# A feed-forward layer in two phases, its inner operands kept in DRAM between, both products by seven block products

## The chip, the cores and the metric

The kernel runs on one core of a Trainium2 chip. The metric is the device time of one launch in microseconds (us), median of the runs. Engines: TensorE (PE, with its weight load PEld), VectorE (DVE), ScalarE (ACT), GpSimd (POOL) and SyncE (SP), which issues all transfers here.

## The reference

One step of a streaming encoder layer on 1024 prompt rows and 64 sample rows (T = 1088 columns), width D = 1024, inner width 4096:

```
z  = x @ w_in
merged = sigmoid(g_A) * y_A + sigmoid(g_B) * y_B     # conv branch, mLSTM branch
x1 = LN(ALPHA * x + merged @ w_out)
ff = square(relu(x1 @ w_ff1)) @ w_ff2                # w_ff1 1024x4096, w_ff2 4096x1024
x2 = LN(ALPHA * x1 + ff)
```

Everything is fp32. Only the feed-forward (the line of `ff`) is changed.

## The kernel before

A product in fp32 is made of three matmuls on operands split into a high and a low part (`mm3`, lines 342, 345, 346: high·high, high·low, low·high). `split` (L350, L353; with a scale L355, L356) makes the parts: ScalarE copies the high part, VectorE takes the difference as the low part. Activations lie with features on the partitions and the 1088 columns in three chunks of 384, 384 and 320. `x1` is held split (X1H, X1L), the kept sum for the second norm is `Y2`, one tile a chunk.

A *unit* is 128 inner features: `unit` makes for each chunk 8 products (24 matmuls) and passes the result to a function `post`. A list of jobs (`J` with a weight piece, `N` without) is worked off in order; `wload` issues a weight piece two jobs ahead, `wsplit` splits it one job ahead. A scheduler then places the instructions on each engine in an order of its own; each engine, and SyncE with its transfers, runs strictly in that order and waits where an operand is not there.

The feed-forward goes over 8 blocks of four units. In blocks 0 to 6, four units of x1 @ w_ff1 (`post_r`: relu, square, and the seven sums that the second product needs, split, kept in SBUF) are followed by the second product for these 512 inner features by seven block products in place of eight (`wino_pair`): operands are cut into halves, sums of halves of weights (`wino_weights`) and of activations are multiplied, and VectorE adds the results into `Y2`. Four passes `jp` over the output features give 4 × 7 × 2 × 2 × 3 = 336 matmuls of 272 columns a block. Both products of a block so alternate with the next block's. Block 7 is classical: `post_h` keeps its four units in SBUF, `y2_turn` transposes `Y2` (L1084, 72 transposes), and `last_ff2` makes the products of 512 columns with the rows as partitions, with the second norm (`ln2_back`) and the stores. The first norm `ln1` runs chunk by chunk beside the first units (`ln_feature`, L744, L745, L748); `first_units` works chunk-wise so that the units can begin before the norm's last chunk is there.

## Time and profile before

| | |
|---|---|
| Time, median of 3 runs | 1944.36 us (1944.29 to 1945.13) |
| The profiled execution | 1945.67 us, span 1943.9 us, TensorE clock 0.998 |
| TensorE busy | 1922.5 us (99%), 12396 matmuls |
| VectorE / ScalarE / GpSimd busy | 1390.9 / 638.1 / 124.0 us |
| Moved by DMA | 131.06 MB, mean 67 GB/s |
| First unit of the feed-forward | from 1191.56 us |
| First block of the second product | 1240.63 to 1286.44 us |

A row of the groups is: line, engine, operation, output<-inputs, shapes, count | busy us, mean ns of one | idle time of the engine just before them, and the releaser that ended most of it. A row of the timeline begins with its start and its duration in us; the bracket at its end is the idle time before it and what ended it. A row of the windows is a stretch, its length, and for PE, PEld, DVE, ACT and POOL the busy time and the count of instructions, then the granted TensorE clock, the DMA share and GB/s. The rows of GB/s and of PEclk cut their stretch into 40 equal slices.

### The profile page before, as it was taken

How to read it: one execution, taken by the hardware profiler on the slowest of the kernel's cores; microseconds unless marked ns; L12 is line 12 of the kernel's file. 1: busy time of each engine (PE TensorE's matmuls, PEld its weight loads, DVE VectorE, ACT ScalarE, POOL GpSimd, SP SyncE). 2: the span in 40 equal slices, each digit the busy share in tenths (PEclk: the TensorE clock that was granted, in tenths of full speed). 3: DMA queues.
4: the chain of work that ended last, by engine and by line, in shares of the span. 5: the costliest groups of instructions: out<-in, count | busy, mean ns of one | idle time of the engine just before them, and what ended most of it. 6: DMA issues, size and time to landing. Idle time of an engine off the chain costs nothing.

```text
span 1943.9 us, 30514 instructions
## 1 busy us (share of the span) xinstructions
PE 1922.5 (99%) x12396; PEld 1902.4 (98%) x12396; DVE 1390.9 (72%) x2735; ACT 638.1 (33%) x1204; POOL 124.0 (6%) x229
## 2 busy tenths in 40 slices
PE   8999999999999999999999999999999999999998
PEld 8999999999999999999999999999999999999996
DVE  4957876787678867877775557868685858677647
ACT  4323322332233223323452214523233232414242
POOL 1112210001000100000000000000000000000005
PEclk9999999999999999999999999999999999999999
DMA  4121311122112211226335211011111111111212
GB/s 144 53 80 52 124 53 53 51 72 57 56 33 68 73 56 44 61 88 198 104 111 155 77 39 39 23 55 45 55 42 46 55 44 47 41 55 44 73 37 92
DMA packets 171744, 131.06 MB, mean 67 GB/s; under 512 B 8271, under 2 KB 166463, under 8 KB 171603
## 3 DMA queue, kind: packets, MB, share of 16 engines
q1 hardware_dynamic: 171603, 129.11, 21.9%
q8 instruction: 97, 1.59, 0.3%
q14 instruction: 44, 0.36, 0.1%
HBM read 104.39 MB, written 24.63 MB: 66 GB/s over the span
## 4 chain that ended last, share of the span: by engine, by line
PE 94%; DVE 4%; DMA 1%; ACT 0%; issue 0%; POOL 0%; DVEq 0%; SPq 0%; POOLq 0%; ACTq 0%
PE g L342 29%; PE g L345 29%; PE g L346 29%; PE m L342 1%; PE m L346 1%; PE m L345 1%; DVE acc L586 1%; PE m L480 0%; PE m L1084 0%; PE m L427 0%; DVE wl L353 0%; PE m L486 0%; PE m L464 0%; DMA x<-in_x_prompt_dram 0%; PE m L169 0%
## 5 line engine op out<-in xcount | busy, mean ns | idle before, releaser
L342 PE MATMUL g<-xh,wh 128*128 128x384 f32 (+1 forms) x1920 | 634.9, 331 | 0.0
L345 PE MATMUL g<-xl,wh 128*128 128x384 f32 (+1 forms) x1920 | 628.9, 328 | 0.9 <-DVE xl L174 0.9
L346 PE MATMUL g<-xh,wl 128*128 128x384 f32 (+1 forms) x1920 | 628.6, 327 | 0.0
L345 PEld LDWEIGHTS g<-xl,wh 128*128 128x128 f32 x1920 | 361.4, 188 | 1.3 <-DVE xl L174 1.2
L342 PEld LDWEIGHTS g<-xh,wh 128*128 128x128 f32 x1920 | 361.3, 188 | 0.7 <-ACT xh L173 0.3
L346 PEld LDWEIGHTS g<-xh,wl 128*128 128x128 f32 x1920 | 361.0, 188 | 0.1
L586 DVE SCALAR_TENSOR_TENSOR acc<-glu,vecs,acc 128x1118 f32<-128x1118 f32 x240 | 332.4, 1385 | 3.6
L350 ACT ACTIVATE wh<-wr 128x1024 fp32r<-128x1024 f32 (+1 forms) x168 | 165.9, 988 | 440.4 <-PE g L345 358.5
L353 DVE TENSOR_TENSOR wl<-wr,wh 128x1024 fp32r<-128x1024 f32 (+1 forms) x168 | 192.7, 1147 | 97.4 <-ACT wh L350 94.5
L342 PE MATMUL g<-x1h,wh 128*128 128x384 f32 (+1 forms) x768 | 252.8, 330 | 0.0
L345 PE MATMUL g<-x1l,wh 128*128 128x384 f32 (+1 forms) x768 | 252.2, 328 | 0.0
L346 PE MATMUL g<-x1h,wl 128*128 128x384 f32 (+1 forms) x768 | 252.1, 328 | 0.0
L345 PE MATMUL g<-hvl,wh 128*128 128x272 f32 x784 | 224.3, 289 | 0.0
L342 PE MATMUL g<-hvh,wh 128*128 128x272 f32 x784 | 221.8, 291 | 1.5 <-DVE y L995 1.5
L346 PE MATMUL g<-hvh,wl 128*128 128x272 f32 x784 | 222.4, 289 | 0.0
L997 DVE TENSOR_TENSOR y<-g,y 128x272 f32<-128x272 f32 (+1 forms) x540 | 156.9, 339 | 28.1 <-PE g L346 26.3
L342 PEld LDWEIGHTS g<-hvh,wh 128*128 128x128 f32 x784 | 146.5, 190 | 3.4 <-DVE y L995 1.9
L345 PEld LDWEIGHTS g<-hvl,wh 128*128 128x128 f32 x784 | 148.1, 189 | 0.0
L346 PEld LDWEIGHTS g<-hvh,wl 128*128 128x128 f32 x784 | 147.1, 189 | 0.0
L345 PEld LDWEIGHTS g<-x1l,wh 128*128 128x128 f32 x768 | 144.3, 188 | 0.1
L342 PEld LDWEIGHTS g<-x1h,wh 128*128 128x128 f32 x768 | 144.2, 188 | 0.1
L346 PEld LDWEIGHTS g<-x1h,wl 128*128 128x128 f32 x768 | 144.3, 188 | 0.0
(276 smaller groups left out, 2359.2 us busy)
## 6 DMA issues: line engine op xcount, KB each, us to landing
wr<-in_w_in_dram SPq DMA_DIRECT2D x64, 512.0 KB
wr<-in_w_ff_dram SPq DMA_DIRECT2D x64, 512.0 KB
x<-in_x_prompt_dram SPq DMA_DIRECT2D x8, 512.0 KB
dwT<-acc SPq DMA_DIRECT2D x8, 512.0 KB
wr<-in_w_b_out_dram SPq DMA_DIRECT2D x8, 512.0 KB
wr<-in_w_a_out_dram SPq DMA_DIRECT2D x8, 512.0 KB
wr<-in_w_out_dram SPq DMA_DIRECT2D x8, 512.0 KB
out_dram<-o SPq DMA_DIRECT2D x16, 256.0 KB
```

What stands on the lines that cost most here:

```text
L342: first = TE.matmul(out, lh, rh, start=start, stop=False, skip_group_check=more)
L345: TE.matmul(out, lh, rl, start=False, stop=False, skip_group_check=more)
L346: TE.matmul(out, ll, rh, start=False, stop=stop, skip_group_check=more)
L350: a = S.activation(hi, src, AF.Copy)
L353: V.tensor_tensor(lo, src, hi.bitcast(F32), ALU.subtract)
L586: V.scalar_tensor_tensor(acc, glu[:, j:j + AC], vecs[:, c, j:j + 1], acc, ALU.mult, ALU.add))
L997: V.tensor_tensor(y, ps[:, pslc], y, ALU.add)
```

## The change

The feed-forward is no longer worked off in blocks that do both products.

- The four classical units (28 to 31) come first; `post_h` writes their two parts to DRAM (`hidD`). `ln1` also writes `Y2`, X1H and X1L to DRAM (`y1D`, `x1D`).
- `x1_sums` makes the four sums of column halves and row blocks of x1 that seven products need, split: six pieces of four sums, four copies and four lows, interleaved with the last chunk's work.
- `ff_first` makes the 28 other units in 14 rounds of seven block products, each 24 matmuls of 272 columns. The three plain operands come back from `x1D`. Weights of a round are loaded raw (1 MB, one buffer), and summed and split form by form (`item`) into nine slots. `stream` sets the order: a round's last three products (P6, P7, P4) stand between the next round's first ones. `done` takes results out of PSUM, makes relu and square, and the seven operands of the second product in two parts, written to DRAM (`hvD`, 14 tiles of 128x544 a round).
- All of that memory is given back; `ff_second` then makes 28 rounds (7 blocks × 4 passes `jp`) of seven products, 84 matmuls of 272 columns each. The operands of a block are read back from `hvD` (14 loads, two blocks' worth of buffers), the kept sum stays in SBUF (`YF`, from `y1D`). `last_ff2` transposes `YF` row tile by row tile between its products, its weights and `hidD` come in during block 5.

The diff, cut to its core:

```diff
-    for blk in range(NBLK - 1):
-        for kt in range(2):
-            for kh in range(2):
-                c0 = (blk * NB + 2 * kh + kt) * P
-                if blk == 0 and kt == 0:
-                    J(wcols(w_ff1[0], c0), lambda hi, lo, kh=kh: first_units(kh, hi, lo), "f" if kh else "w")
-                else:
-                    add_unit(w_ff1[0], c0, lambda *a, kt=kt, kh=kh: post_r(kt, kh)(*a))
-        for jp in range(KT // 2):
-            wino_pair(blk, jp)
...
-    N(open_last)
-    for u in range((NBLK - 1) * NB, NBLK * NB):
-        add_unit(w_ff1[0], u * P, post_h(u))
-    N(last_ff2)
...
+    y1D = dram.tile([D, T], F32, name="y1D")
+    x1D = [dram.tile([D, T], F32, name=f"x1D{e}") for e in "hl"]
+    hidD = [dram.tile([4 * P, T], F32, name=f"hidD{e}") for e in "hl"]
+    hvD = dram.tile([14 * 7 * 2 * P, 544], F32, name="hvD")
...
         yield from ln_feature(Y2[ci], n, pools["ln1"], square, finish, ((2, 3, 2), (1, 3, 1), (1, 2, 1))[ci], YS[ci])
+        o = CHUNKS[ci][0]
+        for dst, src in ((y1D, Y2[ci]), (x1D[0], X1H[ci].bitcast(F32)), (x1D[1], X1L[ci].bitcast(F32))):
+            nc.sync.dma_start(dst[:, o:o + n].rearrange("(k p) t -> p k t", p=P), src[:, :, :n])
...
+    VN = ("b11", "b21", "b22", "t1", "t2", "t3", "t4")
+    USES = {"P1": ("a11", "b11"), "P2": ("a12", "b21"), "P3": ("s4", "b22"), "P5": ("s1", "t1"), "P6": ("s2", "t2"),
+            "P7": ("s3", "t3"), "P4": ("a22", "t4")}
+    BANK = {"P1": "a", "P6": "a", "P7": "a", "P4": "a", "P5": "b", "P3": "b", "P2": "c"}
...
+    def ztile(name):
+        zq.append(0)
+        return pools["hvs1" if len(zq) % 14 < 4 or "hvs2" not in pools else "hvs2"].tile([P, HT2], F32R, tag="z", name=name)
...
+            r, hi = ztile("r"), ztile("rh")
+            rf = r.bitcast(F32)
+            S.activation(rf[:, :n], ps[:, :n], AF.Relu)
+            V.scalar_tensor_tensor(rf[:, :n], ps[:, :n], 0.0, rf[:, :n], ALU.max, ALU.mult)
+            split(hi[:, :n], r[:, :n], rf[:, :n])
+            for e, t in enumerate((hi, r)):
+                nc.sync.dma_start(hidD[e][u * P:(u + 1) * P, o:o + n], t.bitcast(F32)[:, :n])
...
+    def x1_sums():
...
+        for a, b, ca, oa, cb, ob in ((0, 224, 0, 0, 1, 160), (224, 384, 0, 224, 2, 0), (384, 544, 1, 0, 2, 160)):
+            n = b - a
+            for i in range(2):
...
+                V.tensor_tensor(z[0], b11, b12, ALU.subtract)
+                keep("t1", z[0])
+                V.scalar_tensor_tensor(z[1], z[0], -1.0, b22, ALU.mult, ALU.subtract)
+                keep("t2", z[1])
+                V.tensor_tensor(z[0], b22, b12, ALU.subtract)
+                keep("t3", z[0])
+                V.scalar_tensor_tensor(z[1], z[1], -1.0, b21, ALU.mult, ALU.subtract)
+                keep("t4", z[1])
+                yield
...
+        if u == 1:
...
                 unit(*h, (1,))
             early[1] = product(*his[third], 1)
             drain("misc")
+            BG["misc"].append(x1_sums())
+            step("misc")
...
+    N(open_ff)
+    for u in range(4):
+        c0 = (4 * KT - 4 + u) * P
+        if u < 2:
+            J(wcols(w_ff1[0], c0), lambda hi, lo, u=u: first_units(u, hi, lo), "f" if u else "w")
+        else:
+            add_unit(w_ff1[0], c0, post_h(u))
...
+    def stream(n, weight, operand, nk, done, between=None):
...
+            for sg in range(2):
+                for k in range(nk):
+                    bh, bl = operand(q, bn, k, slice(sg * HB, (sg + 1) * HB))
+                    mm3(ps[:, sg, :HB], *weight(q, an, k), bh, bl, nm in ("P1", "P2", "P5") and k == 0, k == nk - 1, more=True)
+            done(q, nm, {k: bank.get((q, k)) for k in "abc"})
+
+        for q in range(n + 1):
+            for nm in ("P6", "P1", "P7", "P5", "P4", "P2", "P3"):
+                old = nm in ("P6", "P7", "P4")
+                if 0 <= q - old < n:
+                    run(q - old, nm)
+                    if between:
+                        between(q - old, nm)
...
+    def ff_first():
...
+        for i, (nm, kh, th) in enumerate((("b11", 0, 0), ("b22", 1, 1), ("b21", 1, 0))):
...
+                nc.sync.dma_start(t.bitcast(F32), x1D[e].rearrange("(i b p) t -> b p i t", b=2, p=P)[kh][:, :, th * HT2:(th + 1) * HT2])
...
+        ws = [fp.tile([P, 3072], F32R, tag="f", name="wv") for _ in range(3)]
+        order = ("a11", "s1", "a12", "s4", "s2", "s3", "a22")
...
+        def produce():
+            for q in range(NQ):
+                raw = pools["rawp"].tile([P, 2 * KT * P], F32R, tag="raw", name="raw").bitcast(F32)
+                nc.sync.dma_start(raw.rearrange("p (k n) -> p k n", n=2 * P),
+                                  w_ff1[0][:, q * 2 * P:(q + 1) * 2 * P].rearrange("(k p) n -> p k n", p=P))
...
+                def item(nm, src):
+                    n = made[0] % 9
...
+                    split(hi, lo, src)
+                    slot_of[q, nm] = (hi, lo)
+                    made[0] += 1
+                item("a11", c[0, 0])
+                V.tensor_tensor(c[0, 0], c[0, 0], c[1, 0], ALU.add)
+                yield
+                V.tensor_tensor(c[1, 0], c[1, 0], c[1, 1], ALU.add)
+                item("s1", c[1, 0])
+                yield
+                item("a12", c[0, 1])
+                yield
+                V.tensor_tensor(tmp, c[0, 0], c[1, 1], ALU.add)
...
+                item("s4", c[0, 1])
...
+        def more(ahead):
+            while made[0] < 7 * NQ:
...
+                if made[0] >= ahead:
+                    return
+                next(gen)
...
+        def put(q, nm, hi, lo):
+            for e, t in enumerate((hi, lo)):
+                o = ((q * 7 + VN.index(nm)) * 2 + e) * P
+                nc.sync.dma_start(hvD[o:o + P, :], t.bitcast(F32))
...
+        def relu2(t, src, scale):
+            S.activation(t, src, AF.Relu, scale=scale)
+            S.activation(t, t, AF.Square)
...
+        def low(q, nm):
+            V.tensor_tensor(Z[nm], f32(nm), Z[nm + "h"].bitcast(F32), ALU.subtract)
+            put(q, nm, Z[nm + "h"], Z[nm])
+
+        def done(q, nm, bk):
+            if nm == "P1":
+                Z["T1"] = ztile("T1")
+                S.activation(halves(f32("T1")), cols2(bk["a"]), AF.Copy)
+            elif nm == "P5":
+                Z["T5"] = ztile("T5")
+                S.activation(halves(f32("T5")), cols2(bk["b"]), AF.Copy)
+            elif nm == "P2":
+                Z["b11"] = ztile("r11")
+                V.tensor_tensor(halves(f32("b11")), cols2(bk["c"]), halves(f32("T1")), ALU.add)
+                relu2(f32("b11"), f32("b11"), 1.0)
+                high("b11")
+            elif nm == "P3":
+                Z["T3"] = ztile("T3")
+                S.activation(halves(f32("T3")), cols2(bk["b"]), AF.Copy)
+            elif nm == "P6":
+                Z["r12"] = ztile("r12")
+                V.tensor_tensor(halves(f32("r12")), cols2(bk["a"]), halves(f32("T3")), ALU.add)
+                relu2(f32("r12"), f32("r12"), 1.0)
+                Z["t1"] = ztile("t1")
+                V.tensor_tensor(f32("t1"), f32("b11"), f32("r12"), ALU.subtract)
+                low(q, "b11")
+            elif nm == "P7":
+                Z["b22"] = ztile("r22")
+                V.tensor_tensor(halves(f32("b22")), cols2(bk["a"]), halves(f32("T5")), ALU.add)
+                relu2(f32("b22"), f32("b22"), -1.0)
+                Z["t3"] = Z["r12"]
+                V.tensor_tensor(f32("t3"), f32("b22"), f32("t3"), ALU.subtract)
+                Z["t2"] = ztile("t2")
+                V.scalar_tensor_tensor(f32("t2"), f32("t1"), -1.0, f32("b22"), ALU.mult, ALU.subtract)
+                for v in ("b22", "t1", "t3"):
+                    high(v)
+                    low(q, v)
+            elif nm == "P4":
+                Z["b21"] = ztile("r21")
+                relu2(halves(f32("b21")), cols2(bk["a"]), -1.0)
+                Z["t4"] = ztile("t4")
+                V.scalar_tensor_tensor(f32("t4"), f32("t2"), -1.0, f32("b21"), ALU.mult, ALU.subtract)
+                for v in ("t2", "b21", "t4"):
+                    high(v)
+                    low(q, v)
...
+        def between(q, nm):
+            used.add((q, USES[nm][0]))
+            count[0] += 1
+            more(count[0] + 8)
+
+        stream(NQ, lambda q, an, k: tuple(t[:, k, :] for t in slot_of[q, an]),
+               lambda q, bn, k, cs: tuple(t[:, k, cs] for t in XV[bn]), 4, done, between)
+        ff1b.close()
+        ff1.close()
+        base.close()
+
+    N(ff_first)
...
+    def ff_second():
...
+        def split_w(q):
...
+            split(part(hi, 0, 4), part(lo, 0, 4), raw.rearrange("p (t n) -> p t n", n=2 * P)[:, :, 0:P])
+            split(part(hi, 4, 2), part(lo, 4, 2), c[1, 1])
+            V.tensor_tensor(c[0, 0], c[0, 0], c[1, 0], ALU.add)
...
+            split(hi[:, 6 * P:], lo[:, 6 * P:], raw)
...
+        def load_hv(blk):
+            for nm in ("b11", "t1", "b21", "b22", "t2", "t3", "t4"):
...
+                    nc.sync.dma_start(t.bitcast(F32), hvD[o:o + 2 * P, :].rearrange("(e p) t -> p e t", p=P))
...
+        def done(q, nm, bk):
+            blk, jp = divmod(q, 4)
...
+                if m == nm:
+                    y = halves(YF[jp][:, mh, th * HT2:(th + 1) * HT2])
+                    op = ALU.subtract if mh else ALU.add
...
+        def between(q, nm):
+            if nm == "P5":
+                load_w(q + 3)
+                split_w(q + 2)
+            if nm == "P4" and q % 4 == 3:
+                blk = q // 4
+                if blk + 2 < 7:
+                    load_hv(blk + 2)
+                if blk == 5:
+                    stacks[1].close()
+                    last_weights()
+
+        load_hv(0)
+        load_w(0)
+        load_w(1)
+        for j in range(4):
+            nc.sync.dma_start(YF[j], y1D[j * 2 * P:(j + 1) * 2 * P, :].rearrange("(b p) t -> p b t", p=P))
+        split_w(0)
+        split_w(1)
+        load_w(2)
+        load_hv(1)
+        stream(nq, weight, operand, 2, done, between)
+        banks.close()
+        ff2.close()
+        last_ff2(YF)
...
+    def last_weights():
...
+            split(WH[k], WL[k], raw)
+            HID[k] = [la.tile([P, TW], F32R, name=f"hid{k}{e}") for e in "hl"]
...
+    def last_ff2(YF):
...
+        def turn(i):
...
+                for k in range(4):
+                    j = 4 * kh + k
+                    TE.transpose(p[:n, k * P:(k + 1) * P], YF[j // 2][:, j % 2, i * P:i * P + n], ident)
+                S.activation(yt[:n, kh * 512:(kh + 1) * 512], p[:n], AF.Copy)
+            return yt
...
+        nxt = turn(0)
...
+                    mm3(p, hh[:, i * P:(i + 1) * P], hl[:, i * P:(i + 1) * P], WH[k][:, hs], WL[k][:, hs], k == 0, k == 3)
+                if hf == 0 and i + 1 < NT:
+                    nxt = turn(i + 1)
+                V.tensor_tensor(y[:, hs], p[:n], y[:, hs], ALU.add)```

Three places in the engines' orders. `hid` tiles are the classical units' squares, `xb` the reloaded operands of x1, `raw` the weights of a round of the first stream, `hv` the operands of the second stream, `yf` the kept sums, `wr` weights, `xs` and `xt` the sums of x1 and their parts, `r` and `rh` a unit's square and its high part, `wv` weight forms.

SyncE's transfers behind the first norm, before: only weights.

```order
L858 DMA sx<-xTD 128x320 x8
L1151 DMA wr<-in_w_ff_dram 128x4x256 x4
L1151 DMA wr<-in_w_ff_dram 128x8x128 x4
L1151 DMA wr<-in_w_ff_dram 128x4x256 x4
L1151 DMA wr<-in_w_ff_dram 128x8x128 x4
```

The same place after, at the end of the four units:

```order
L922 DMA hidDh<-rh 128x320
L922 DMA hidDl<-r 128x320
L1024 DMA xb_12495<-x1Dh 128x4x544
L922 DMA hidDh<-rh 128x384
L922 DMA hidDl<-r 128x384
L922 DMA hidDh<-rh 128x384
L922 DMA hidDl<-r 128x384
L1024 DMA xb_12497<-x1Dl 128x4x544
L922 DMA hidDh<-rh 128x320
L922 DMA hidDl<-r 128x320
L1037 DMA raw<-in_w_ff_dram 128x8x256 x2
```

The raw weights of the first two rounds stand behind the last store of the last unit.

SyncE after, between the first and the second stream (there was no such place before):

```order
L1090 DMA hvD<-zh 128x544
L1090 DMA hvD<-t_16073 128x544
L1225 DMA hv<-hvD 128x2x544 x14
L1262 DMA yf_16127<-y1D 128x2x1088
L1262 DMA yf_16128<-y1D 128x2x1088
L1186 DMA wr<-in_w_ff_dram 128x4x256
L1225 DMA hv<-hvD 128x2x544 x14
L1186 DMA wr<-in_w_ff_dram 128x4x256 x2
L1225 DMA hv<-hvD 128x2x544 x2
```

The weights of rounds 0 and 1 were issued earlier; those of round 2 stand behind block 0's operands and two kept sums, those of rounds 3 and 4 behind block 1's operands.

VectorE behind the norm's last chunk, before:

```order
L353 TENSOR_TENSOR x1l<-y_11582,x1h 128x2x320 x3
L927 SCALAR_TENSOR_TENSOR r<-g,r 128x2x160
L935 TENSOR_TENSOR t<-r 128x544
L353 TENSOR_TENSOR hvl<-r,hvh 128x544
L927 SCALAR_TENSOR_TENSOR r<-g,r 128x2x160
```

and after, the last of the six pieces of `x1_sums` and what follows it:

```order
L359 TENSOR_TENSOR xt1l<-xs,xt1h 128x2x160
L948 TENSOR_TENSOR xs<-y_11588 128x320
L359 TENSOR_TENSOR xt2l<-xs,xt2h 128x2x160
L950 SCALAR_TENSOR_TENSOR xs<-xs,y_11289 128x320
L359 TENSOR_TENSOR xt3l<-xs,xt3h 128x2x160
L359 TENSOR_TENSOR xt4l<-xs,xt4h 128x2x160
L919 SCALAR_TENSOR_TENSOR r<-g,r 128x384
L359 TENSOR_TENSOR r<-r,rh 128x384
L919 SCALAR_TENSOR_TENSOR r<-g,r 128x384
L359 TENSOR_TENSOR r<-r,rh 128x384
L919 SCALAR_TENSOR_TENSOR r<-g,r 128x320
L359 TENSOR_TENSOR r<-r,rh 128x320
L359 TENSOR_TENSOR wv<-raw,wv 128x512 x2
```

The last unit's square and low, from which the last `hid` store is made, stand behind the sums and their lows; the weight forms of the first round follow.

More of the change, by code (lines that the diff above doesn't have):

```diff
@@ L846, in ln1 @@
             lns.close()
-            pools["hw0"] = pool("hw0", 1, stack=win)
     def out_proj():
@@ new lines, in hybrid_layer, with rows, keep @@
+    XV = {}
+    def x1_sums():
+        tv = pools["tv"] = pool("tv", 1, stack=ff1)
+        for nm in ("t1", "t2", "t3", "t4"):
+            XV[nm] = [tv.tile([P, 4, HT2], F32R, tag=nm + e, name="x" + nm + e) for e in "hl"]
+        def rows(kh, i, ci, o, n):
+            return Y2[ci][:, 4 * i + kh:4 * i + 4:2, o:o + n]
+        for a, b, ca, oa, cb, ob in ((0, 224, 0, 0, 1, 160), (224, 384, 0, 224, 2, 0), (384, 544, 1, 0, 2, 160)):
+            n = b - a
+            for i in range(2):
+                b11, b21, b12, b22 = rows(0, i, ca, oa, n), rows(1, i, ca, oa, n), rows(0, i, cb, ob, n), rows(1, i, cb, ob, n)
+                z = [ztile("xs").bitcast(F32)[:, :2 * n].rearrange("p (k t) -> p k t", t=n) for _ in range(2)]
+                def keep(nm, src):
+                    hi, lo = (t[:, 2 * i:2 * i + 2, a:b] for t in XV[nm])
+                    split(hi, lo, src)
[8 more added lines that the diff above has]
+                yield
@@ L1017, in first_units @@
+    def first_units(u, hi, lo):
+        post = post_h(u)
         unit(hi, lo, post, (0,))
         held.append((hi, lo, post))
-        if kh == 1:
-            pools["whl"] = pools["whl2"]
+        if u == 1:
             third = 2 + next(i for i, p in enumerate(pieces) if p[3] == 1)
-            wsplit(third)
+            w3 = pools["rawp"].tile([P, 2 * KT * P], F32R, tag="raw", name="w3")
+            h3, l3 = w3[:, 0:KT * P], w3[:, KT * P:]
+            split(h3, l3, raws[third])
+            his[third] = tuple(t.rearrange("p (k n) -> p k n", n=P) for t in (h3, l3))
@@ L1073, in y2_turn @@
-    def y2_turn():
-        for ci in range(3):
-            if ci == 0:
-                YT.append(pools["ln2"].tile([P, 3, D], F32, tag="yt", name="yt", bufs=1))
-            else:
-                YT.append(fp.tile([P, 3, D], F32, tag="f", name="yt"))
-            for t in range(3):
-                n = tile_len(3 * ci + t)
-                for kh in range(2):
-                    ps = mtile()
-                    for k in range(4):
-                        TE.transpose(ps[:n, k * P:(k + 1) * P], Y2[ci][:, 4 * kh + k, t * P:t * P + n], ident)
-                    S.activation(YT[ci][:n, t, kh * 512:(kh + 1) * 512], ps[:n], AF.Copy)
-                yield
```

320 lines of the change are left out of this document (153 added, 167 removed).

## The prediction

> **What bounds the kernel now.** I read the page first, then the matmuls of the feed-forward by shape, then the starts of its stages on the PE timeline, then what stands on the other engines there.
>
> ```profile
> span 1943.9 us, 30514 instructions
> PE 1922.5 (99%) x12396; PEld 1902.4 (98%) x12396; DVE 1390.9 (72%) x2735; ACT 638.1 (33%) x1204; POOL 124.0 (6%) x229
> PEclk9999999999999999999999999999999999999999
> PE 94%; DVE 4%; DMA 1%; ACT 0%; issue 0%; POOL 0%; DVEq 0%; SPq 0%; POOLq 0%; ACTq 0%
> L342 PE MATMUL g<-hvh,wh 128*128 128x272 f32 x784 | 221.8, 291 | 1.5 <-DVE y L995 1.5
> L342 PE MATMUL g<-x1h,wh 128*128 128x384 f32 x512 | 173.5, 339 | 0.0
> L342 PE MATMUL g<-x1h,wh 128*128 128x320 f32 x256 | 79.3, 311 | 0.0
> L342 PE MATMUL g<-w2h,hh 128*128 128x512 f32 x72 | 28.4, 396 | 0.0
> ```
>
> TensorE is busy for 99% of the span, at full clock, and carries 94% of the chain of waits; the last four rows (one of each set of three matmuls of a product) show idle time before them of 1.5 us in all. So a matmul taken away is worth its whole pitch, and each new wait of TensorE costs its whole length. A matmul's "mean ns" overlaps the next one, so I take pitches from starts:
>
> ```profile
> 1240.63 0.29 PE L342 MATMUL g<-hvh,wh 128*128 128x272 f32 x1
> 1286.44 0.34 PE L342 MATMUL g<-x1h,wh 128*128 128x384 f32 x1
> 1376.76 0.34 PE L342 MATMUL g<-x1h,wh 128*128 128x384 f32 x1
> 1424.64 0.28 PE L342 MATMUL g<-hvh,wh 128*128 128x272 f32 x1
> 1467.08 0.34 PE L342 MATMUL g<-x1h,wh 128*128 128x384 f32 x1
> ```
>
> Four units of the first product (288 matmuls) take 1424.64 − 1376.76 = 47.88 us, 11.97 us a unit. One block of the second (336 matmuls of 272 columns) takes 1467.08 − 1424.64 = 42.44 us, 0.1263 us each. The very first block took 1286.44 − 1240.63 = 45.81 us, 3.37 us more.
>
> **The gain.** The change makes 28 of 32 units (7/8 of the first product) by seven block products. Before: 28 × 11.97 = 335.2 us. After: 14 rounds × 7 products × 24 matmuls = 2352 matmuls of 272 columns, × 0.1263 = 297.1 us. That is −38.1 us. The second product has the same 2352 matmuls before and after; the 3.37 us of its late first block I count as gone, since any new delay at its start is counted below. The last four units, the last classical product, the 72 transposes and the tail keep their work. Gain: −41.5 us. Everything else is waiting.
>
> **The start of the first stream.** The new operands need 24 sums of x1 on VectorE, each followed by a copy on ScalarE and a difference on VectorE, and they stand in VectorE's order among the last of the four units' own steps. SyncE issues all transfers in order, and the weights of round 0 stand behind the last unit's last store, which waits for VectorE to come through. Prices:
>
> ```profile
> 1213.55 0.31 PE L745 MATMUL m<-sl,ones 128*128 128x320 f32 x1
> 1217.91 0.31 PE L342 MATMUL g<-x1h,wh 128*128 128x320 f32 x1
> 1213.89 0.82 DVE L748 TENSOR_TENSOR y<-y,m 128x640 f32<-128x640 f32 x1 [1.59 <-PE m L745]
> 1226.35 0.48 DVE L927 SCALAR_TENSOR_TENSOR r<-g,r 128x320 f32<-128x320 f32 x1
> 1226.75 0.72 DVE L353 TENSOR_TENSOR hvl<-t,hvh 128x544 fp32r<-128x544 f32 x1
> 1227.38 0.72 DVE L944 TENSOR_TENSOR t<-r 128x544 f32<-128x544 f32 x1
> 1231.20 0.55 DVE L927 SCALAR_TENSOR_TENSOR r<-g,r 128x384 f32<-128x384 f32 x1
> 1231.67 0.71 DVE L946 TENSOR_TENSOR t<-t,r 128x544 f32<-128x544 f32 x1
> 1234.74 0.68 DVE L353 TENSOR_TENSOR wl<-wr,wh 128x512 fp32r<-128x512 f32 x1
> 1235.34 0.55 DVE L353 TENSOR_TENSOR hvl<-t,hvh 128x384 fp32r<-128x384 f32 x1
> 1880.96 4.12 DMA wr<-in_w_ff_dram
> ```
>
> From start to start VectorE takes 0.40 us for 320 elements, 0.47 for 384, 0.60 for 512, 0.63 for 544; for 448 I put 0.54 between them. Let B be the moment of the third row, when the last column chunk of the layer norm is let through. TensorE's chunk-2 work starts at B + 4.0 (second row); it has this chunk of three units (320 of 1088 columns, 11.97 × 320/1088 = 3.52 each, 10.6) and a whole unit of 11.97 to do; with 0.9 for waits on the norm, which now does more (below), it runs dry at about B + 27.5. VectorE behind B has: the sums and their lows, 16 instructions of 448 and 32 of 320, 16 × 0.54 + 32 × 0.40 = 21.4; twelve-odd steps of the units' squares and lows, some 7; the x1 lows of the norm, 3; a weight low, 1. That is 32.5 us without a gap, and about 40 if gaps like the 1.59 us ahead of the third row (VectorE waiting for another engine) take a fifth of the time. Then comes the load of 1 MB: a lone 512 KB took 4.12 us (last row), another 512 KB at 360 GB/s (row below) adds 1.5, and the first split some 1.2: the first product at about B + 47, a wait of 19.5 us. Bounds: if VectorE holds nothing up, the last unit's own store and the load alone remain, 7 us; with wider gaps 25.
>
> Behind a wait the clock drops:
>
> ```profile
> 1250.09 0.38 PE L346 MATMUL g<-hvh,wl 128*128 128x272 f32 x1
> 1250.26 0.43 PE L342 MATMUL g<-hvh,wh 128*128 128x272 f32 x1
> 1250.49 0.43 PE L345 MATMUL g<-hvl,wh 128*128 128x272 f32 x1
> 1252.98 0.43 PE L345 MATMUL g<-hvl,wh 128*128 128x272 f32 x1
> 1253.21 0.57 PE L346 MATMUL g<-hvh,wl 128*128 128x272 f32 x2
> ```
>
> For 3 us after small gaps near 1247 and 1249, fourteen matmuls ran at 0.227 us in place of 0.126: 1.5 us lost, and I put 1.7 behind each long wait (0 to 3). First start: +21.
>
> **The rounds of the first stream.** A round has 168 matmuls, 21.2 us. VectorE has 25 instructions in it: 14 of 544 and 11 of 512 elements, 14 × 0.63 + 11 × 0.60 = 15.4 us; ScalarE 25 of like size, 15 us at 0.6 (from a row below). Each round writes 14 tiles of 278 KB (3.9 MB) and reads 1.05 MB: 4.95 MB in 21.2 us, 233 GB/s. How a like load was borne before:
>
> ```profile
> 1339.60:1381.80 42.20, 42.20 (x326) 42.17 (x326) 34.36 (x104) 7.68 (x10) 0.00 (x0) 1.00 0.20 59
> 1381.90:1429.60 47.70, 47.70 (x299) 47.56 (x297) 30.20 (x69) 20.88 (x46) 0.00 (x0) 1.00 0.12 37
> GB/s 0 0 0 0 0 0 0 0 41 0 0 0 0 0 0 0 0 0 0 18 141 364 369 358 62 0 0 0 0 0 0 0 0 0 0 0 0 0 0 0
> GB/s 0 0 0 110 125 214 313 431 417 389 423 410 437 403 414 359 321 297 177 114 60 232 437 376 416 430 423 417 423 348 340 310 360 137 55 7 27 20 48 20
> ```
>
> The first row is a block of the second product: VectorE busy 34.36 of 42.20 us (81%) and TensorE without a gap; the second a group of the first. The third is a weight load of 512 KB in 16 us, slices of 0.4 us; the last the first 24 us of the kernel, 389 to 437 GB/s where transfers queue. So 15.4 of 21.2 us (73%) of VectorE and 233 GB/s fit. The sixth, seventh and fourth products add to one accumulation bank, with another product (3.0 us) between each two, in which VectorE must have read the bank (0.63). I cost the rounds at 0 to 5 us, and take 1. The stream's end has no other product between its last three: each waits for VectorE's addition of the one before, about 0.9 us, twice: +1.8 (1 to 3).
>
> **The start of the second stream.** All pools of the first stream close, and SyncE's order is: the last stores, the 14 loads of block 0 (14 × 557,056 bytes = 7.80 MB), two of the four kept sums (2.23 MB), the weights of round 2 (0.52), the 14 loads of block 1 (7.80), and only then the weights of round 3 (0.52): 18.87 MB. With T the last product's end: behind it come two activations for the square, a difference, and three copies and lows one behind the other, all of 544 elements:
>
> ```profile
> 1226.87 1.21 ACT L350 ACTIVATE hvh<-r 128x544 fp32r<-128x544 f32 x2 [0.32 <-DVE r L927]
> ```
>
> At 0.6 for each activation (row) and 0.63 on VectorE that is 1.2 + 0.6 + 3 × 0.6 + 0.6 = 4.2, and with hops and the last store's issue 5.4 us (3.5 to 7) until block 0's loads begin. At 400 GB/s, between the 358 of the third row and the 437 of the fourth, 18.87 MB take 47.2 us; with 0.8 to first data and 1.5 for landing and split, round 3 can begin at about T + 55. Ahead of it TensorE has only 19 products of 12 matmuls, 19 × 12 × 0.1263 = 28.8 us, and where these wait for block 0 lies inside the same time. A wait of 26.2, with the clock +28. At 358 GB/s it is 52.7 us and +33; at 437, 43.2 and +24. If the loads of block 1 held up nothing, block 0's arrival at T + 5.4 + 0.8 + 19.5 = 25.7 against the 12.1 us of work ahead of its last operand would leave 13.6, with the clock +15.
>
> The Trainium skill ("DMA: Bandwidth & Descriptors", Specifications) gives about 358 GB/s as the limit between HBM and one core. The fourth row, 437 GB/s, exceeds it, so the measurement decides; by the page the term would be an estimated +33.
>
> **The rounds of the second stream.** VectorE does 7 additions of 544 (4.4 us) and the weights of a round (lows of 512, 256 and 1024, four sums of 256: about 3.3), 7.7 of 10.6 us, 73%, against the 81% above; one block is 9.9 MB per 42.4 us, again 233 GB/s. 0 to 8, taken 1. Its end: two waits for additions and one before the transposes, +2.8 (2 to 4). The last product begins with 8 transposes and a copy that lay beside other work: +1. In the norm, sums and squares of the new kind stand between its own VectorE steps: −0.5 to 3, taken 0.9, the wait that is inside B + 27.5: +1.
>
> **Sum.** −41.5 + 21 + 1 + 1.8 + 28 + 1 + 2.8 + 1 + 1 = +16.1 us. The profiled execution took 1945.67 us (span 1943.9 and 1.8 around it), 1.3 above the median of 1944.36. 1944.4 + 16.1 = 1960.
>
> **The rivals.**
> *The queue holds nothing up, and it is faster.* If SyncE's order costs nothing at either start, only the first operands count: 7 + 1.7, and 13.6 + 1.7. With the other 8.6 of the sum that makes 32.6 of waits against 41.5 of gain: −8.9, 1935. It decides where the two starts together fall below 33. For it speaks that 16 engines carry the transfers; against it that VectorE's 32.5 us stand in the order ahead of the store, and that 18.9 MB must move. If one start alone is short, it ends near 1944, no change.
> *Rounds stretched.* Each reader of a bank stands in VectorE's line behind weight splits and lows that themselves wait for ScalarE. One lost us in each of 14 rounds and a half in each of 28 give +28, half of it +14: 1974 to 1988. For it: bursts of 4 us of VectorE work behind one product. Against: 81% without a gap before.
> *Transfers at the lower row's rate.* With 358 GB/s throughout, the second start gives +33 and the first a little more: 1966.
> *Transfers cannot hold 233 GB/s in both streams*, since stores and loads share the engines. At 200, 14 × (24.7 − 21.2) + 6 × (49.5 − 42.4) = +91: 2050. No row before shows stores at this rate for long; the first 24 us show twice it for loads.
>
> **How the numbers follow.** Both starts as worked out: 0.52 (own range 1949 to 1972). Rate of 358: 0.10 (1966). Rounds stretched: 0.12. Too few GB/s: 0.03. Nothing held up: 0.14. One start short: 0.09. Likeliest: 1960. All bounds at their good end, 7 and 14 for the starts, give 1926, all at their bad end 1985. The range leaves out most of the first rival and the last one: 1941 to 1982. About 0.2%, 3.9 us, can be told from no change: faster 0.14, same 0.09, slower 0.77.
>
> **What would show it.** Right: TensorE without work for about 20 us between the last unit and the first block product, then half clock for 3 us; rounds of 21.2 us; a second hole of 25 us or more spread over the first four rounds of the second stream, its last part ended by the weights of round 3; blocks of 42.4 us after it. Wrong: holes under 10 us; VectorE named as releaser in every round; a pitch of 272 columns other than 0.126; moved GB/s below 233 in the streams.

## The result and the profile after

The changed kernel takes 1974.13 us (median of 4 runs, 1973.22 to 1974.54) against 1944.74 us before: 29.4 us slower, ratio 1.015 (95% interval 1.0132 to 1.0168). The forecast was 1960 us, slower by 16, with a range of 1941 to 1982: the direction and the range held, the loss was nearly twice the forecast.

The page of the changed kernel, the same rows as of before:

```profile
span 1972.4 us, 31778 instructions
PE 1893.3 (96%) x12732; PEld 1869.6 (95%) x12732; DVE 1420.7 (72%) x2332; ACT 711.8 (36%) x1277; POOL 124.1 (6%) x229
PEclk9999999999999999999999999799999989999999
GB/s 143 53 79 67 110 61 44 45 78 49 55 48 74 59 55 33 67 102 209 89 123 141 68 112 166 281 184 245 231 224 247 254 397 283 214 258 251 168 104 81
PE 81%; DVE 9%; DMA 7%; issue 1%; ACT 1%; SPq 0%; POOL 0%; DVEq 0%; ACTq 0%; POOLq 0%
```

TensorE is busy for 29 us less than before (1922.5) and the span is 28.5 us longer. The chain of waits, 94% TensorE before, now holds 9% VectorE and 7% transfers. Two slices of the clock show 7 and 8, and the transfers run at 184 to 397 GB/s from slice 26 to 37, where they were 23 to 73. What TensorE waited for from 1150 us to the end (engine, line, releaser: us in total, times, longest):

```profile
PE ya L348 <- ACT wv L356: 28.0, 1, 28.0
PE ya L348 <- DMA hv<-hvD: 13.0, 1, 13.0
PE ya L348 <- DVE yf L1244: 4.8, 5, 1.5
PE ya L348 <- ACT wh L356: 4.7, 1, 4.7
PE g L348 <- DVE y L872: 4.1, 1, 4.1
```

Before, this view has 2.0 us in all from 1191 us on. The starts of the stages on the PE timeline:

```profile
1186.39 0.63 PE L348 MATMUL g<-xh,woh 128*128 128x320 f32 x1 [4.14 <-DVE y L872]
1199.92 0.34 PE L348 MATMUL g<-x1h,wh 128*128 128x384 f32 x1
1277.45 0.59 PE L348 MATMUL ya<-xb,wv 128*128 128x272 f32 x1 [27.98 <-ACT wv L356]
1577.61 0.29 PE L352 MATMUL ya<-xt4h,wv 128*128 128x272 f32 x1
1590.86 0.57 PE L348 MATMUL ya<-hv,wh 128*128 128x272 f32 x1 [12.97 <-DMA hv<-hvD]
1637.15 0.59 PE L348 MATMUL ya<-hv,wh 128*128 128x272 f32 x1 [4.66 <-ACT wh L356]
1906.82 0.38 PE L1304 MATMUL pt<-ident,yf 128*128 128x128 f32 x2
```

From these rows and those of before:

| Stage | before | after | difference | forecast |
|---|---|---|---|---|
| Output projection and norm, start of the first unit | 1191.56 | 1199.92 | +8.4 | +1 |
| Four classical units | 49.1 | 49.4 (to 1249.30) | +0.3 | 0 |
| Hole before the first stream | | 28.1 | +28.1 | +19.5 |
| 28 units; first stream, 1277.45 to 1577.74 | 335.2 | 300.3 | −34.9 | −38.1 + 1.8 + 1 + 1.7 = −33.6 |
| Hole between the streams | | 13.1 | +13.1 | |
| Second product; second stream, 1590.86 to 1906.82 | 297.1 + 3.4 | 316.0 | +15.5 | |
| Both together | | | +28.6 | 28 + 1 + 2.8 − 3.4 = +28.4 |
| Last product with its 72 transposes, and the tail (before: what is left of the span) | 67.6 | 65.6 | −2.0 | +1 |

The differences add to 28.5 us, that of the spans. The steady parts went as worked out (length, then PE, PEld, DVE, ACT, POOL busy, clock, DMA share, GB/s):

```profile
1300.00:1540.00 240.00, 239.84 (x1908) 239.00 (x1907) 181.39 (x283) 163.35 (x282) 0.00 (x0) 1.00 0.64 233
1680.00:1889.00 209.00, 209.00 (x1673) 209.00 (x1672) 165.69 (x277) 40.96 (x60) 1.09 (x8) 1.00 0.63 227
```

In both streams TensorE has work without a gap, at full clock, with VectorE 76% and 79% busy and 233 and 227 GB/s moved. The 38 us are gained; nearly all of the loss lies at three starts.

### The profile page after: what moved, and what is told of

It is laid out like the page before. It is cut to its first block, busy times and chain, and to the rows that moved or that the text cites. A ratio compares the mean times of both kernels' runs of the same rounds, so it can differ in the third digit from the quotient of the medians.

```text
span 1972.4 us, 31778 instructions
## 1 busy us (share of the span) xinstructions
PE 1893.3 (96%) x12732; PEld 1869.6 (95%) x12732; DVE 1420.7 (72%) x2332; ACT 711.8 (36%) x1277; POOL 124.1 (6%) x229
## 4 chain that ended last, share of the span: by engine, by line
PE 81%; DVE 9%; DMA 7%; issue 1%; ACT 1%; SPq 0%; POOL 0%; DVEq 0%; ACTq 0%; POOLq 0%
PE g L348 17%; PE g L351 17%; PE g L352 17%; PE ya L348 4%; PE ya L352 4%; PE ya L351 4%; DMA raw<-in_w_ff_dram 2%; PE yb L348 2%; PE yb L352 2%; PE yb L351 2%; DMA hv<-hvD 1%; PE m L352 1%; PE m L348 1%; PE m L351 1%; PE yc L348 1%
## 5 line engine op out<-in xcount | busy, mean ns | idle before, releaser
L348 PE MATMUL g<-xh,wh 128*128 128x384 f32 (+1 forms) x1920 | 634.3, 330 | 0.1
L352 PE MATMUL g<-xh,wl 128*128 128x384 f32 (+1 forms) x1920 | 628.3, 327 | 0.0
L348 PEld LDWEIGHTS g<-xh,wh 128*128 128x128 f32 x1920 | 360.5, 188 | 0.9 <-ACT xh L179 0.4
L352 PEld LDWEIGHTS g<-xh,wl 128*128 128x128 f32 x1920 | 360.3, 188 | 0.1
L356 ACT ACTIVATE wh<-wr 128x1024 fp32r<-128x1024 f32 (+1 forms) x167 | 144.0, 877 | 428.7 <-PE g L351 168.6
L359 DVE TENSOR_TENSOR wl<-wr,wh 128x1024 fp32r<-128x1024 f32 (+1 forms) x167 | 167.0, 1013 | 67.5 <-ACT wh L356 66.6
L348 PE MATMUL ya<-hv,wh 128*128 128x272 f32 x448 | 131.3, 294 | 23.4 <-DMA hv<-hvD 13.0
L352 PE MATMUL ya<-hv,wl 128*128 128x272 f32 x448 | 130.1, 291 | 0.5 <-DVE wl L359 0.5
L351 PE MATMUL ya<-hv,wh 128*128 128x272 f32 x448 | 129.7, 290 | 0.0
L348 PEld LDWEIGHTS ya<-hv,wh 128*128 128x128 f32 x448 | 85.9, 192 | 25.8 <-issue 13.2
L1244 DVE TENSOR_TENSOR yf<-yf,ya 128x544 f32<-128x544 f32 x100 | 70.1, 718 | 39.4 <-PE ya L352 39.1
L352 PEld LDWEIGHTS ya<-hv,wl 128*128 128x128 f32 x448 | 85.4, 191 | 0.8 <-DVE wl L359 0.7
L351 PEld LDWEIGHTS ya<-hv,wh 128*128 128x128 f32 x448 | 85.5, 191 | 0.0
L359 DVE TENSOR_TENSOR wv<-raw,wv 128x512 fp32r<-128x512 f32 x84 | 56.2, 686 | 38.1 <-ACT wv L356 37.7
L356 ACT ACTIVATE wv<-raw 128x512 fp32r<-128x512 f32 x84 | 51.0, 623 | 59.9 <-DMA raw<-in_w_ff_dram 53.9
L348 PE MATMUL g<-xh,woh 128*128 128x384 f32 (+1 forms) x192 | 63.9, 333 | 4.1 <-DVE y L872 4.1
L348 PE MATMUL yb<-hv,wh 128*128 128x272 f32 x224 | 65.0, 290 | 1.1 <-ACT wh L356 1.0
L352 PE MATMUL yb<-hv,wl 128*128 128x272 f32 x224 | 64.5, 288 | 0.5 <-DVE wl L359 0.5
L351 PE MATMUL yb<-hv,wh 128*128 128x272 f32 x224 | 64.3, 287 | 0.0
```

The costliest lines, as they stand in the source:

```text
L348: first = TE.matmul(out, lh, rh, start=start, stop=False, skip_group_check=more)
L351: TE.matmul(out, lh, rl, start=False, stop=False, skip_group_check=more)
L352: TE.matmul(out, ll, rh, start=False, stop=stop, skip_group_check=more)
L356: a = S.activation(hi, src, AF.Copy)
L359: V.tensor_tensor(lo, src, hi.bitcast(F32), ALU.subtract)
L1244: V.tensor_tensor(y, y, cols2(bk[b]), op)
```

## The experiments

In most of the experiments' kernels one or more transfers change their place or their queue. Profiles of the same work differ by more than 2 us already ahead of the feed-forward (the units' last matmul starts at 1249.15 in the changed kernel and at 1251.45 in e1, which differ only behind it), so beside the median I compare the length of the stage.

### What the reloads of x wait for

The place where 4.1 us are lost before the first unit, on SyncE's timeline:

```profile
1153.42 0.32 SPq L866 DMA_DIRECT2D sx<-xTD  x1
1170.84 0.37 SPq L852 DMA_DIRECT2D y1D<-y  x1
1171.72 0.37 SPq L852 DMA_DIRECT2D x1Dh<-x1h  x1
1173.14 0.55 SPq L852 DMA_DIRECT2D x1Dl<-x1l  x1
1173.73 13.43 SPq L866 DMA_DIRECT2D sx<-xTD  x6
```

and in the chain of waits (start, us, what):

```profile
1173.73 12.09 DMA sx<-xTD
```

The three rows from 1170.84 are chunk 0's norm stores, 3 × 1.57 = 4.7 MB. The last reloads of x, which the output projection adds, stand behind them in SyncE's order, and this delays them twice. From 1153.42 on SyncE stands still until the first store has its data, and the first of the reloads then lands 12.09 us after its issue, behind the 4.7 MB. Before, the last six reloads go out from 1161.43 on:

```profile
1161.43 15.32 SPq L858 DMA_DIRECT2D sx<-xTD  x6
```

Behind the wait the clock is down: it is 0.50 from 1186.39 to 1191.90 in the profile. The matmuls stand 0.267 us apart there, against 0.147 at full clock, which loses some 2.5 us more.

```diff
-            nc.sync.dma_start(dst[:, o:o + n]..., src[:, :, :n])
+            for kh in range(2):
+                nc.gpsimd.dma_start(dst[512 * kh:512 * kh + 512, o:o + n]..., src[:, 4 * kh:4 * kh + 4, :n])
```

> The norm's copies of Y2, X1H and X1L to DRAM (nine transfers, each cut in two) are issued by GpSimd instead of SyncE; the same bytes move. Theory A (the reloads of x stand behind 4.7 MB of stores in one queue): the wait of 4.1 us in the output projection and the slow clock behind it are gone, the first unit begins near 1192 to 1194 us instead of 1199.9, the kernel takes about 1967 us. Rival B (the stores take the 16 engines' time whatever queue they are in): the first unit still begins after 1198, and the time is 1972 to 1976.

1976.93 us (1973.33 to 1977.75), ratio to before 1.0163 (1.0148 to 1.0178): no gain. The wait for the reload is gone, and a longer one stands in its place. GpSimd's timeline:

```profile
1189.33 0.76 POOL L853 DMA_DIRECT2D x1Dl<-x1l  x1 [3.30 <-issue]
1193.38 0.76 POOL L853 DMA_DIRECT2D x1Dl<-x1l  x1 [3.30 <-issue]
1194.16 0.88 POOL L742 TENSOR_TENSOR ln<-ln,mhalf 128x3 f32<-128x3 f32 x1
```

and TensorE's waits:

```profile
PE m L750 <- ACT sh L356: 10.8, 1, 10.8
```

GpSimd needs 4.05 us for each of these issues, and the norm's own step on it (L742, the inverse root) comes behind them, with the step of ScalarE that TensorE waits for behind that. Neither theory is borne out: the first unit begins at 1205.65, in rival B's range, but for this other reason. The reload is no longer waited for once the stores have left SyncE's queue; GpSimd was the wrong place for them. The hole before the first stream is shorter than in the changed kernel, since the scheduler also issued round 0's weights earlier here (at 1243.76 in place of 1269.87), and it is 19.7 us long in place of 28.1. So the issues cost more than the medians show.

```diff
-            nc.sync.dma_start(dst[:, o:o + n]...)          # on e6 (below)
+            nc.scalar.dma_start(dst[:, o:o + n]...)
```

> As the kernel before in this list, and the norm's nine stores are issued by ScalarE instead of SyncE (whole, not cut). Theory A (the reload of x stands behind 4.7 MB of stores in one queue, and GpSimd was the wrong queue because the norm's own step on it had to wait): first unit at 1193 to 1195 us, 6 us gained, about 1947 us. Rival B (the 16 engines serve the stores all the same, or ScalarE in its turn is held up by the issues): no gain, 1952 us or more.

1977.24 us (1976.06 to 1979.17), ratio 1.0166 (1.0152 to 1.018), 15.7 us slower than e6, its base. TensorE's waits:

```profile
PE m L736 <- ACT sh L356: 6.8, 2, 3.5
PE yb L348 <- ACT T L1124: 6.8, 1, 6.8
PE m L750 <- ACT sh L356: 2.8, 1, 2.8
```

Again TensorE has no wait for the reload of x, and waits for ScalarE. In the norm, ScalarE's steps stand behind its issues: between its second issue (1172.20) and its third (1176.79) it does nothing else, and the square in the first row below comes only after it. The 6.8 us in the first stream's first round are another matter: the step T stands behind weight forms that waited for their weights to land (second row).

```profile
1177.20 1.49 ACT L727 ACTIVATE sq<-y 128x1536 f32<-128x1536 f32 x1 [5.03 <-DMA y1D<-y]
1290.90 1.15 ACT L356 ACTIVATE wv<-raw 128x512 fp32r<-128x512 f32 x2 [5.09 <-DMA raw<-in_w_ff_dram]
```

Rival B, in its second half: ScalarE is held up by the issues.

```diff
-            store_x1(0)      # at the end of ln1(0); on e6
+        if ci == 2:          # in out_proj
+            drain("misc")
+            store_x1(0)
```

> As the kernel with the last stores on ScalarE's queue, and the norm's stores stay on SyncE, but those of chunk 0 are written behind the last reloads of x in the program (in SyncE's order one of the three stores still stands ahead of four reloads of chunk 2, a second ahead of two). Theory A (bytes ahead of the reloads): 1.6 to 3.1 MB instead of 4.7 MB stand ahead, the wait of 5.8 us there shrinks to 0 to 2, about 1948 us. Rival B: the stores push the units' own first stores back and the hole before the first stream grows by as much, 1952 us or more.

1955.21 us (1953.79 to 1957.53) against e6's 1961.55, ratio to before 1.0055 (1.0042 to 1.0067): 6.3 us gained. The wait in the projection is gone, the units' last matmul starts at 1243.43 instead of 1250.34, and the hole that follows is the same as e6's (16.3). The four late reloads are issued at nearly the time of the changed kernel (1173.73), but with one store of 1.57 MB just ahead of them in place of three:

```profile
1172.50 0.37 SPq L859 DMA_DIRECT2D y1D<-y  x1
1172.92 3.81 SPq L870 DMA_DIRECT2D sx<-xTD  x4
```

Theory A: the cost is the bytes ahead of a needed reload in one queue, and it goes when most of them are put behind it. In e2 and e7 the same stores were issued by another engine, at the same place of the program, and the wait for the reload was gone as well; so the place in SyncE's queue makes it, and not the stores as such.

### The first stream's start

```diff
-            add_unit(w_ff1[0], c0, post_h(u))
+            J(wcols(w_ff1[0], c0), lambda hi, lo, u=u: (first_raw(), unit(hi, lo, post_h(u))))   # u == 3
...
-                raw = pools["rawp"].tile(...); nc.sync.dma_start(raw, ...)
+                raw = RAW0.pop() if q == 0 else load_raw(q)
```

> The load of round 0's weights for the first stream is issued at the start of the last unit instead of behind its last store. Theory A (VectorE's line, then the load and the split, one behind the other): the load's 6.9 us leave the hole, the first block product begins 6 to 7 us earlier, hole 21 to 22 us instead of 28, kernel about 1967.5 us. Rival B (the transfers of the place as a whole are the bound, so that one pulled ahead pushes the others back): hole 26 us or more, 1972 to 1974.

1965.89 us (1965.53 to 1969.95), ratio 1.0115 (1.01 to 1.013): 8 us gained, the hole 16.9 us in place of 28.1, more than theory A had. The releaser is another one now:

```profile
PE ya L348 <- DVE r L919: 16.7, 1, 16.7
PE ya L348 <- DVE r L1135: 4.0, 5, 1.3
```

The first product no longer waits for its weights but, by the releaser named, for VectorE to read a unit's result out of an accumulation bank (L919). Some of the gain is given back: in the profile the stream is 306.4 us long in place of 300.3, with waits in its first rounds (second row). This profile is of the slowest of the four runs, 1969.95; in e5 and e11, which have this edit too, the stream is 304.4 and 304.1 us long, so some 4 us are given back.

```diff
+            if nm != "t1":
+                for t in XV[nm]:
+                    G.memset(t.bitcast(F32), 0.5)
...
                 keep("t1", z[0])
-                V.scalar_tensor_tensor(z[1], z[0], -1.0, b22, ALU.mult, ALU.subtract)
-                keep("t2", z[1])
-                ...
```

> Leaves out three of the four sums of x1: their operands are filled with a constant by GpSimd, so VectorE and ScalarE do a quarter of that work (the output is another). Theory A (VectorE's line holds up the last unit's store and with it the weights): 16 us of VectorE work are gone and the hole shrinks from 28 to 11 to 14 us, kernel about 1959 us. Rival B (stores and reloads of x1 are the bound there): the hole stays at 23 us or more, kernel 1969 to 1974.

1974.31 us (1973.74 to 1976.34), ratio 1.0155 (1.014 to 1.017): nothing. The hole is 26.9 us, though 18 sums and 18 lows are gone. The chain of waits there:

```profile
1236.07 6.98 DMA hidDh<-rh
1250.67 5.45 DMA hidDh<-rh
1263.89 11.60 DMA raw<-in_w_ff_dram
```

and on VectorE's timeline:

```profile
1243.15 0.49 DVE L947 TENSOR_TENSOR xs<-y,y 128x320 f32<-128x320 f32 x1 [4.61 <-DMA hidDh<-rh]
```

VectorE, no longer behind with its own work, waits for units' stores to land, since the four `z` buffers are shared by the units' results and the sums (4.61 us in the row above, and 4.08 us once more); these stores stand behind the 3.9 MB of chunk 2's norm stores and the reloads. The weights were issued 6 us earlier than in the changed kernel (1263.89 against 1269.87) and took 11.60 us in place of 6.87, behind two reloads of 1.1 MB issued just ahead. So VectorE's line and the queue look like two bounds of nearly the same length there, and taking away one moves the wait to the other; this is argued from e3 and e4, and no run takes both away. Both runs speak against my forecast's view that VectorE alone set this start.

```diff
+        for _ in x1_sums(False):      # t2, t3, t4, behind more(6); t1 stays among the units
+            pass
```

> Both reorderings, chunk 0's norm stores behind the reloads of x, SyncE for all stores, and of the sums of x1 only the first kind (which the second block product needs) is made among the units; the other three kinds follow behind the first weight forms. Theory A (with the weights early, the last unit's steps on VectorE behind the sums hold the first stream up: TensorE waits for VectorE to read that unit's accumulation bank): these steps come some 10 us earlier, hole before the first stream 4 to 8 us in place of 16 to 17, kernel 1943 to 1947 us. Rival B (moved work is paid in the first round, or the reloads of x1 take its place): hole shorter but waits of as much in the first two rounds, 1951 us or more.

1957.76 us (1957.51 to 1959.89), ratio 1.0067 (1.0053 to 1.0081). Against the kernel with the same orders of transfers but the sums in their old place (e11, 1952.84) it is 4.9 us slower: hole 24.5 in place of 16.6. The scheduler put these sums ahead of the first weight forms on VectorE, and VectorE waited 4.69 us on the way for a store of a unit and 5.40 us for a copy of ScalarE, which itself waited for one:

```profile
1259.02 0.47 ACT L356 ACTIVATE rh<-r 128x320 fp32r<-128x320 f32 x1 [5.68 <-DMA hidDl<-r]
```

The time lies in rival B's range, but not as told there: the hole did not get shorter, it grew.

### The second stream's start

```diff
         load_w(2)
-        load_hv(1)
...
                 load_w(q + 3)
                 split_w(q + 2)
+                if q == 0:
+                    load_hv(1)
```

> Only the order of transfers at the start of the second stream changes: block 1's 14 operand loads (7.8 MB) are written behind the weights of round 3 instead of ahead of them. Theory A (TensorE waits for the weights of round 3 because of their place in SyncE's order): the wait of 4.8 us ahead of round 3 and the ones that lead to it shrink, the start of the second stream costs 18 to 20 us instead of 28, and the kernel takes about 1965 us against 1974. Rival B (the start is bound by the 18.9 MB themselves): the wait moves to the first round of block 1, and the time stays at 1972 to 1976.

1970.83 us (1968.44 to 1972.71), ratio 1.0135 (1.0118 to 1.0152): 3.3 us gained by the medians. The single wait of 4.7 us for weights (ACT wh, in the changed kernel) is gone from TensorE's waits; the second stream is 309.0 us long in place of 316.0, and from the first stream's last product to the end of the span it takes 388.3 in place of 394.8, 6.5 us less; 2.6 of it are lost ahead of the change's place, at 1580.23 against 1577.61. So the start costs 13.4 + 309.0 − 297.1 − 3.7 (the end's waits) = 21.6 us in place of 28.3: theory A, short of its size (18 to 20 us, about 1965).

> Both reorderings together: round 0's weights for the first stream loaded at the start of the last unit, block 1's operands behind the weights of round 3. Theory A (two separate places): the gains add, hole before the first stream 17 to 20 us in place of 28, start of the second stream some 22 us in place of 28, about 1960 us. Rival B (one transfer budget, given back later): 1965 us or more.

1960.42 us (1959.19 to 1961.66), ratio 1.008 (1.0066 to 1.0094). Both edits of e1 and e3 together. They bring 13.7 us, more than the 11.5 of the medians of each: theory A, two separate places.

```diff
-                nc.sync.dma_start(hvD[o:o + P, :], t.bitcast(F32))
+                (nc.scalar if q == NQ - 1 else nc.sync).dma_start(hvD[o:o + P, :], t.bitcast(F32))
```

> As the kernel with both reorderings, and the last round's 14 operand stores of the first stream are issued by ScalarE, so that SyncE can go on to block 0's loads. Theory A (the 7.9 us from the last block product to block 0's first load are the place behind those stores in SyncE's order): the hole of 13.1 us between the streams shrinks to 4 to 7 us, 7 us gained, about 1953 us. Rival B (the memory that block 0's operands take over comes free only when those stores have read it): the hole stays at 11 us or more, 1958 us or more.

1961.55 us (1960.53 to 1962.79), ratio 1.0086 (1.0072 to 1.01), no gain on e5, and the hole between the streams grew from 12.9 to 17.2 us. The chain there:

```profile
1572.41 9.05 DMA hvD<-t
1581.47 6.58 DMA hv<-hvD
```

Block 0's first load is issued when one of the last stores has landed, 9.05 us after its issue by ScalarE: the loads wait for these stores, most likely because they fill memory that the stores still read (argued, not shown apart). With SyncE free, the loads of the four kept sums (4.5 MB, from 1561.00 on) went out ahead and the stores landed later. Rival B. Only the high parts on ScalarE:

> As the kernel before, and of the last round's stores of the first stream the seven high parts are issued by ScalarE, the low parts by SyncE. Theory A (SyncE needs 0.6 us for each of 12 stores issued one behind the other): block 0's loads start 2 to 4 us earlier, hole between the streams 9 to 11 us instead of 13. Rival B (the loads wait for the stores to land, since their memory is taken over): hole 13 us or more, no gain.

1961.66 us (1960.0 to 1966.05), ratio 1.0088 (1.0074 to 1.0102), and 20.1 us of hole against 14.0 of e9, its base. That is rival B's size, but not its reason: the chain goes through the loads of the four kept sums, which again went out ahead of block 0's.

```profile
1571.28 11.40 DMA yf<-y1D
```

So e6 and e10 moved two things at once, the stores and the kept sums; stores moved with the kept sums left behind block 0 were not tried.

### Together, and VectorE's line once more

> Only orders of transfers on SyncE are changed: round 0's weights earlier, block 1's operands later, chunk 0's norm stores behind the reloads of x. Theory A (three separate waits, each from the place of a transfer in one queue): gains of some 8, 6 and 7 us add up, hole before the first stream 16 to 17 us, between the streams 13, kernel 1952 to 1955 us. Rival B (what is taken from the norm is given back before the first stream): 1958 us or more.

The edits of e1, e3 and e8 without that of e6: 1952.84 us (1952.1 to 1954.39), ratio 1.0043 (1.0029 to 1.0056): of 29.4 us, 21.3 are won back by three orders of transfers and nothing else, theory A. What remains:

```profile
PE ya L348 <- DVE r L924: 16.4, 1, 16.4
PE ya L348 <- DMA hv<-hvD: 12.8, 1, 12.8
PE ya L348 <- DVE yf L1260: 5.1, 5, 1.8
```

It is the fastest of the changed kernels and still 8 us slower than before. On top of it, all 24 sums of x1 on GpSimd:

```diff
-                V.tensor_tensor(z[0], b11, b12, ALU.subtract)
+                G.tensor_tensor(z[0], b11, b12, ALU.subtract)
...
```

> As the kernel before in this list, and the 24 sums of x1 are made by GpSimd, which is idle there; VectorE keeps the 24 lows. Theory A (VectorE's line of 45 us between the norm's last chunk and the last unit's square holds the first stream up once the weights are early): some 11 us of VectorE work are gone, hole before the first stream 6 to 10 us in place of 16, kernel 1944 to 1948 us. Rival B (the waits for the units' stores to land, or GpSimd's own slower sums, take its place): hole 13 us or more, 1951 us or more.

1961.84 us (1961.5 to 1965.93), ratio 1.0092 (1.0078 to 1.0106): 9 us slower than e11, hole 21.7. The same lows on VectorE (busy us, mean ns) in e11:

```profile
L359 DVE TENSOR_TENSOR xt3l<-xs,xt3h 128x320 fp32r<-128x320 f32 x4 | 1.9, 484 | 0.1
L359 DVE TENSOR_TENSOR xt3l<-xs,xt3h 128x448 fp32r<-128x448 f32 x2 | 1.2, 618 | 0.0
```

and in e12:

```profile
L359 DVE TENSOR_TENSOR xt3l<-xs,xt3h 128x320 fp32r<-128x320 f32 x4 | 3.3, 826 | 1.6 <-ACT xt3h L356 1.6
L359 DVE TENSOR_TENSOR xt3l<-xs,xt3h 128x448 fp32r<-128x448 f32 x2 | 2.5, 1257 | 1.8 <-ACT xt3h L356 1.8
```

While GpSimd works, VectorE's instructions take up to about twice as long (618 to 1257 ns), so moving half of the work there shortened nothing, and GpSimd's own sums (0.86 to 2.07 us each) came into the chain. Rival B.

## Why the prediction was right or wrong

**The gain** was right: 28 units cost 335.2 us, the first stream 300.3 with its slow start and its two waits at the end, which were 1.0 and 1.0 us where I had 0.9 each. The late first block of the second product is gone as counted.

**The rounds** were right: no wait in the steady part of either stream, at VectorE's 76 and 79% (forecast 73% each) and 233 and 227 GB/s (forecast 233). The rivals of stretched rounds and of too few GB/s are out.

**The second stream's start** was right in size: 28 with the rounds and the end 2.8, less 3.4, stood against 28.6. Its make-up was nearly as told: 13.1 us to the first product, small waits, and 4.7 us for the weights of round 3. Block 0's loads began 7.9 us after the last product, not 5.4: the last low ended 5.2 us after it, where 4.2 was put, and SyncE then needed until 1585.59 for its remaining stores, 0.6 to 0.7 us each. The sum also left out eleven stores (3.1 MB) issued behind the last product and ahead of the loads; the transfers did not pause while VectorE and SyncE worked:

```profile
1577.74:1590.86 13.12, 0.15 (x2) 0.03 (x1) 11.32 (x21) 6.57 (x11) 0.00 (x0) 0.63 1.00 369
```

Round 3 so began at T + 59.4 where T + 55 was put. That the total still came out is in part luck: the rounds took 10.51 us where 10.61 was put, 2.8 us less over 28 of them. e1 shows block 1's operands ahead of the weights as a cause. e6 shows that a free SyncE gains nothing, since there the loads waited for the last stores to land.

**The start of the first stream** was mis-sized: 21 forecast, 28.1 and the slow clock measured. The step that was mis-sized is the sum over VectorE's line, 32.5 us of work and 7.5 of gaps. From B (1222.26) to the last low VectorE did 39.2 us of work and had 8.0 of gaps:

```profile
1222.26:1269.47 47.21, 26.99 (x168) 26.28 (x166) 39.23 (x75) 27.56 (x55) 0.00 (x0) 0.83 0.78 272
```

I had counted twelve-odd steps of the units' squares and lows where there are 18, and had left out four steps of the norm. So VectorE came through at B + 47, where 40 was put, and from there to the first product it took 8.0 us where 7 was put. The upper end of 25 was still too low. Taking VectorE's line for the only bound was wrong too: in e4, with most of its sums gone, nearly the same hole remained, made of stores, reloads and the weights in one queue.

**The norm** is the step that failed outright: I put +1 there, for VectorE's interleaved sums, and it cost 8.4, of which 4.1 are the wait for the reload and some 2.5 the slow clock behind it; the rest I did not trace. The nine new stores stand in the diff, in `ln1`, and the sum has no term for them; 4.7 MB of them stand ahead of reloads of x in SyncE's order. e8 shows that putting chunk 0's stores behind the reloads takes the cost away.

**The last product** took 2.0 us less than before, where I put +1. Why is not shown.

**The range** held partly by its width: the room above 1960 was there for wider gaps, lower rates and stretched rounds. What filled it was VectorE's longer line (+8.6 on the first hole) and the stores of the norm (+7.4), for which it had no term.

**The rivals.** That the queue holds nothing up was out by 39 us (1935). At the lower transfer rate the forecast was 1966, but the rates were not lower: in the stretches below, while block 0's and block 1's operands came in, the transfers moved 403 and 414 GB/s. This is above the 358 GB/s that the Trainium skill ("DMA: Bandwidth & Descriptors", Specifications) gives as the limit between HBM and one core, as 437 was in the trace before:

```profile
1590.86:1601.47 10.61, 10.41 (x62) 9.59 (x63) 2.88 (x4) 0.00 (x0) 0.00 (x0) 0.82 1.04 403
1601.47:1612.08 10.61, 10.53 (x83) 10.28 (x83) 4.41 (x7) 0.00 (x0) 0.00 (x0) 1.00 1.04 414
```

What stays open: how far the second hole could shrink if block 0's operands had memory of their own, and the first if the units' results and the sums had more than four buffers; neither was tried. Nor were the other norm stores, 3.9 MB of chunk 2 ahead of the units' own stores, moved by themselves.

## What to carry to other kernels

A change that saves work on the bound engine by going through DRAM must be priced at its seams: list for each seam every transfer ahead of the first needed one, in the order of the issuing queue, and do so for all places at which the diff adds a transfer, also those that serve a later stage. Ask of each when its data are ready, since a store that has to wait for them also held up the loads behind it here. A start with two bounds of like length may not move when one is taken away, as in e4. Change the order of transfers first: it cost no work and won back 21.3 of 29.4 us here. Before a queue or an engine is called free, look at what of its own stands behind the moved work and what it shares with its neighbour.

## What the runs showed of the hardware that I had not expected

- While GpSimd made tensor sums of 320 and 448 elements, VectorE's lows of the same sizes went from 484 to 826 and from 618 to 1257 ns (e11 and e12).
- A store of 0.8 MB issued by GpSimd occupies it for 4.05 us from issue to issue (e2), against 0.9 to 1.4 us from one to the next of 1.57 MB on SyncE (rows at 1170.84 to 1173.14).
- How soon a load landed went with what stood ahead of it in the queue: 1 MB of weights took 6.87 us, and 11.60 us with 2.2 MB issued just ahead of it (changed kernel and e4); a reload of x of 164 KB took 12.09 us behind 4.7 MB of stores (changed kernel).
